# Feed-forward stages of a two-layer hybrid block: VectorE, ScalarE and TensorE keep the written order, high parts three steps ahead and low parts two

## Chip, cores and metric

One core of a Trainium2 chip. The metric is the device time of one execution in microseconds, a median of runs. TensorE does the matrix products, VectorE (DVE) and ScalarE (ACT) prepare their operands, the DMA queues of SyncE (SP) and GpSimd (POOL) bring the weights from HBM.

## What is computed

Two layers on 256 rows of 2048 floats. Layer 0 mixes with a gated delta rule and a gated linear recurrence, layer 1 with two kinds of attention; behind each mixer stands a feed-forward stage of width 5632. The part that matters here:

```python
def swiglu(hn, w_gate, w_up, w_down):
    return (jax.nn.silu(hn @ w_gate) * (hn @ w_up)) @ w_down

for layer in range(2):
    h = h + mixer(rmsnorm(h, norm[layer]), ...)
    h = h + swiglu(rmsnorm(h, ffn_norm[layer]), w_gate[layer], w_up[layer], w_down[layer])
return rmsnorm(h, final_norm)
```

## The kernel before

**Two parts.** Every float32 operand is split into a high part (`whi`, `thi`: a rounding copy on ACT, L181 and L378) and a low part (`wlo`, `tlo`: the rest, a subtraction on DVE, L182 and L379). `Bank.add` (L407) multiplies high by high, high by low and low by high: three matmuls for each of two slices of 128 rows, six for a tile of 128 x 1024 weights and one output bank. The second of the six is the first that reads the low part.

**Blocks.** A feed-forward stage is 11 gu blocks (512 columns of gate and up) and 6 dn blocks (1024 output columns), in three pieces: four gu blocks and two dn blocks twice, then three and two. A block (`block`, L421) has *plain* steps, in which one loaded weight tile feeds two banks (12 matmuls), and *sevens*: two by two tiles of a product by seven block products instead of eight. A seven's seven steps have 6 matmuls each; four of them load a tile, three need a sum of tiles `T` on DVE (L386), and the last one's operand is summed by a DMA that adds in flight (L450, POOL). A gu block has 8 plain steps and two sevens (22 steps; the first block of a stage has 16 plain ones); a dn block has one or two sevens.

**Combinations.** A seven also needs sums and differences of its left operand (`comb`, from `combine`, L389): a sum `cf` of high and low part, four differences `cc`, a high and a low part. For dn blocks the left operand is `hid`, the turned product of the gate and up values, so ten combinations, five for each stage, are made in the middle of the stages.

**The end of a block.** `ends` (L471) joins the banks `M` of the sevens in `e`; then the banks `F` are added, ACT applies silu, DVE multiplies; `turn` (L511) lets TensorE transpose the result (8 transposes, `Ph`, L516), ACT rounds (L520), DVE takes the low part (L521), both into `hid`. Dn blocks add to the residual `h`.

**What sets the order.** A scheduler places the instructions of each engine by priorities and its own estimate; the program's order is its input alone. Only the last lines of the kernel are held in the written order. Buffers: high parts 4 + 2, low parts 3 + 2, raw tiles 3 + 4, banks 4 + 4, `T` 2 (shared with `cc`). A stage's names: `P` plain step, `s1` to `s14` the steps of the two sevens of a gu block.

Of the kernel before, what the change touches and what calls it, by code (L numbers as in the profile page):

```python
# [6 lines left out]
ALU = mybir.AluOpType  # L7
# [40 lines left out]
def body(tc, A, out):  # L48
# [340 lines left out]
    def combine(x4, r=None):  # L389

        f = mx.tile([128, 4, T], F32, name="cf", tag="T", bufs=2)
        c = mx.tile([128, 4, 2, 128], F32, name="cc4", tag="T", bufs=2)
        if r is None:
            r = fp.tile([128, 2, 4, 2, 128], F32R, name="comb", tag="comb", bufs=4)
        V.tensor_tensor(out=f, in0=x4[:, :, 0].bitcast(F32), in1=x4[:, :, 1].bitcast(F32), op=ALU.add)
        a11, a21, a12, a22 = (f[:, 2 * j:2 * j + 2, t * 128:(t + 1) * 128] for j in range(2) for t in range(2))
        for i, (x, y) in enumerate(((a21, a22), (a21, a11), (a22, c[:, 1]), (a12, c[:, 2]))):
            V.tensor_tensor(out=c[:, i], in0=x, in1=y, op=ALU.subtract)
        S.copy(r[:, 0], c)
        V.tensor_tensor(out=r[:, 1], in0=c, in1=r[:, 0].bitcast(F32), op=ALU.subtract)  # L400
        return r

# [14 lines left out]
    def sums():  # L417

        return [[mx.tile([128, 512], F32, name=f"e{t}{i}", tag=f"e{t}{i}", bufs=1) for i in range(2)] for t in range(2)]

    def block(src, x, comb, nd, hooks, tail=0, lead=2, trail=None, pairs=False):  # L421
# [49 lines left out]
        def ends():  # L471
            (c1, w5), (v, w7) = sums()
            S.copy(c1, M[0].t)
            for o, a, b, op in ((v, M[2], c1, ALU.subtract), (w5, M[1], v, ALU.add), (v, M[3], v, ALU.add), (w7, M[3], w5, ALU.add)):
                V.tensor_tensor(out=o, in0=a.t, in1=b, op=op)
            return [[c1, w5], [v, w7]]

# [4 lines left out]
        for j, (i, u) in enumerate(plain):  # L482
# [14 lines left out]
            while k < len(sevens) and k < (j - lead + 2) * len(sevens) // gaps:  # L497
                next(sevens[k])
                k += 1
                if k == len(sevens):  # L500
                    e = ends()

                paused[0] = not more and k < len(sevens)
        return [[y.t for y in f] for f in F], e

    def ffn(L, then, fin=None):

        gu, dn = A[f"gu{L}"], A[f"dn{L}"]
        todo, cx, ch = [], {}, {}

        def turn():  # L511
            Ps = []
            for hid, j, t, a in todo:
                P = ms([128, 4, 128], "Ph")
                for i in range(4):
                    PE.transpose(P[:, i], a[:, i * 128:(i + 1) * 128], tb["ident"])  # L516
                Ps.append((P, hid[:, 4 * j:4 * j + 4, :, t * 128:(t + 1) * 128]))
            todo.clear()
            for P, d in Ps:
                S.copy(d[:, :, 0], P)  # L520
                V.tensor_tensor(out=d[:, :, 1], in0=P, in1=d[:, :, 0].bitcast(F32), op=ALU.subtract)  # L521

        b = 0

        for groups in ((0, 2, 2, 2), (2, 2, 2, 2), (2, 2, 2)):
            piece = len(groups)
            hid = ogp.tile([128, 16, 2, T], F32R, name="hid", tag="hid")
            late = {4: lambda hid=hid: ch.update({0: combine(hid[:, 0:4])})}
            for j in range(piece):
                hooks = {2: turn} if todo else {}  # L530
                if b == 0:
                    hooks[5] = lambda: cx.update({0: combine(X[:, 0:4])})
                    hooks[8] = rstd
                    hooks[10] = lambda: cx.update({1: combine(X[:, 4:8])})
                if j == 1 and piece == 3:

                    hooks[6] = late[4]
                F, e = block(lambda i, u: gu[b, u, i], lambda k: X[:, k], {m: lambda m=m: cx[m] for m in range(groups[j])}, 4, hooks)
                a = e or sums()
                for t in range(2):  # L540
                    if e:
                        V.tensor_tensor(out=a[t][0], in0=F[t][0], in1=e[t][0], op=(ALU.add, ALU.subtract)[t])
                    S.activation(a[t][0], a[t][0] if e else F[t][0], AF.Silu, scale=nrm["rs"][:, t:t + 1])
                for t in range(2):
                    if e:
                        V.tensor_tensor(out=a[t][1], in0=F[t][1], in1=e[t][1], op=ALU.add)
                    V.scalar_tensor_tensor(out=a[t][0], in0=a[t][1] if e else F[t][1], scalar=nrm["rs"][:, t:t + 1],
                                           in1=a[t][0], op0=ALU.mult, op1=ALU.mult)
                    todo.append((hid, j, t, a[t][0]))
                b += 1  # L550
            u0 = 2 * (b - piece)
            for p in range(2):
                end = b == NB and p == 1
                hooks = {2: turn} if todo else {}
                if p == 0 and piece == 4:
                    hooks.update(late)

                    hooks[9] = lambda hid=hid: ch.update({1: combine(hid[:, 4:8])})
                if end and fin:
                    hooks.update({5: lambda: then(0), 6: lambda: then(1)})  # L560
                last = (3, 1, 3) if end and fin else (0, 5 if 4 in hooks else 2)
# [761 lines left out]
```

## Time and profile before

| | us |
|---|---|
| median of 3 runs (2222.97 to 2225.14) | 2224.02 |
| the profiled execution | 2222.2 |
| its span | 2220.4 |

What lies around the span is 1.8 us, and the profiled execution is 1.8 us under the median. How to read the rows further down: times are from the span's start; a matmul's end is modelled, so the pace of TensorE is read from the starts of neighbours; "x2" joins neighbours of one kind, and its time reaches from the first one's start to the last one's end.

### The profile page before, as it was taken

How to read it: one execution, taken by the hardware profiler on the slowest of the kernel's cores; microseconds unless marked ns; L12 is line 12 of the kernel's file. 1: busy time of each engine (PE TensorE's matmuls, PEld its weight loads, DVE VectorE, ACT ScalarE, POOL GpSimd, SP SyncE). 2: the span in 40 equal slices, each digit the busy share in tenths (PEclk: the TensorE clock that was granted, in tenths of full speed). 3: DMA queues.
4: the chain of work that ended last, by engine and by line, in shares of the span. 5: the costliest groups of instructions: out<-in, count | busy, mean ns of one | idle time of the engine just before them, and what ended most of it. 6: DMA issues, size and time to landing. Idle time of an engine off the chain costs nothing.

```text
span 2220.4 us, 30372 instructions
## 1 busy us (share of the span) xinstructions
PE 2206.9 (99%) x10984; PEld 1843.7 (83%) x10984; DVE 1946.1 (88%) x2730; ACT 1302.7 (59%) x1708; POOL 50.6 (2%) x62
## 2 busy tenths in 40 slices
PE   9999999999999999999999999999999999999998
PEld 8888888888888888888888888888888888888886
DVE  8899676679999999999996688857999999999998
ACT  6786664555555665556664554445665566555565
POOL 0000000000000000000000000000000000000000
PEclk9999999999999999999999999999999999999999
DMA  8445446677777776787664455556786777777774
GB/s 282 159 144 169 137 150 190 207 221 228 214 225 230 220 230 217 220 235 225 192 201 152 157 185 172 161 188 200 221 232 212 219 231 231 220 214 239 219 238 150
DMA packets 125991, 451.67 MB, mean 203 GB/s; under 512 B 14064, under 2 KB 15600, under 8 KB 125712
## 3 DMA queue, kind: packets, MB, share of 16 engines
q1 hardware_dynamic: 117488, 420.10, 58.4%
q0 software_dynamic: 8064, 29.36, 7.8%
q8 instruction: 86, 1.41, 0.2%
q14 instruction: 65, 0.53, 0.1%
q10 hardware_dynamic: 288, 0.27, 0.0%
HBM read 447.58 MB, written 2.10 MB: 203 GB/s over the span
## 4 chain that ended last, share of the span: by engine, by line
PE 97%; DVE 2%; DMA 1%; issue 1%; ACT 0%; DVEq 0%; ACTq 0%
PE F L413 16%; PE F L414 16%; PE F L412 16%; PE Pw L201 11%; PE Pw L206 6%; PE M L413 5%; PE M L414 5%; PE M L412 5%; PE Px L305 3%; PE Px L306 3%; PE Px L307 3%; PE Ph L516 1%; PE Psc L1088 1%; PE Pt L328 0%; DVE wlo L182 0%
## 5 line engine op out<-in xcount | busy, mean ns | idle before, releaser
L181 ACT CAST whi<-raw 128x1024 fp32r<-128x1024 f32 x717 | 752.3, 1051 | 640.6 <-PE F L414 279.3
L182 DVE TENSOR_TENSOR wlo<-raw,whi 128x1024 fp32r<-128x1024 f32 x717 | 870.9, 1220 | 153.2 <-PE Px L306 40.9
L201 PE MATMUL Pw<-X,whi 128*128 128x512 f32 x1088 | 388.3, 400 | 0.0
L412 PE MATMUL F<-whi,X 128*128 128x512 f32 x934 | 365.4, 391 | 0.0
L413 PE MATMUL F<-wlo,X 128*128 128x512 f32 x934 | 364.0, 390 | 0.0
L414 PE MATMUL F<-whi,X 128*128 128x512 f32 x934 | 363.6, 389 | 0.0
L206 PE MATMUL Pw<-X,wlo 128*128 128x256 f32 x1088 | 304.7, 280 | 0.1
L378 ACT CAST thi<-T 128x1024 fp32r<-128x1024 f32 x177 | 186.0, 1051 | 123.5 <-DVE T L386 89.4
L201 PEld LDWEIGHTS Pw<-X,whi 128*128 128x128 f32 x1088 | 204.1, 188 | 47.2 <-issue 0.5
L379 DVE TENSOR_TENSOR tlo<-T,thi 128x1024 fp32r<-128x1024 f32 x177 | 216.1, 1222 | 30.8 <-ACT thi L378 30.2
L206 PEld LDWEIGHTS Pw<-X,wlo 128*128 128x128 f32 x1088 | 205.3, 189 | 1.5 <-DVE wlo L182 0.7
L414 PEld LDWEIGHTS F<-whi,X 128*128 128x128 f32 x934 | 175.3, 188 | 36.4
L412 PEld LDWEIGHTS F<-whi,X 128*128 128x128 f32 x934 | 175.3, 188 | 35.8
L413 PEld LDWEIGHTS F<-wlo,X 128*128 128x128 f32 x934 | 175.4, 188 | 35.6
L412 PE MATMUL F<-whi,hid 128*128 128x512 f32 x480 | 187.5, 391 | 0.0
L414 PE MATMUL F<-whi,hid 128*128 128x512 f32 x480 | 186.9, 389 | 0.0
L413 PE MATMUL F<-wlo,hid 128*128 128x512 f32 x480 | 186.9, 389 | 0.0
L386 DVE TENSOR_TENSOR T<-T,raw 128x1024 f32<-128x1024 f32 x118 | 143.9, 1219 | 0.8
L413 PE MATMUL M<-tlo,comb 128*128 128x512 f32 x336 | 131.7, 392 | 0.7 <-DVE tlo L379 0.6
L412 PE MATMUL M<-thi,comb 128*128 128x512 f32 x336 | 131.3, 391 | 0.1
L414 PE MATMUL M<-thi,comb 128*128 128x512 f32 x336 | 131.0, 390 | 0.0
L414 PEld LDWEIGHTS F<-whi,hid 128*128 128x128 f32 x480 | 90.1, 188 | 18.7
(403 smaller groups left out, 3281.0 us busy)
## 6 DMA issues: line engine op xcount, KB each, us to landing
raw<-in_gu SPq DMA_DIRECT2D x352, 512.0 KB, 4.4
raw<-in_dn SPq DMA_DIRECT2D x176, 512.0 KB, 4.3
raw<-in_w0w SPq DMA_DIRECT2D x72, 512.0 KB, 3.7
raw<-in_wo SPq DMA_DIRECT2D x64, 512.0 KB, 3.6
raw<-in_w1w SPq DMA_DIRECT2D x64, 512.0 KB, 3.6
raw<-in_gu POOLq DMA_DIRECT2D x40, 512.0 KB, 7.0
raw<-in_w1x SPq DMA_DIRECT2D x32, 512.0 KB, 4.0
raw<-in_w0x SPq DMA_DIRECT2D x16, 512.0 KB, 3.6
```

The lines of the kernel that those rows point to most:

```text
L181: S.copy(hi, raw)
L182: V.tensor_sub(lo, raw, hi.bitcast(F32))
L201: PE.matmul(P.rearrange("p a b -> p (a b)"), hi[:, kk], X[:, k].rearrange("p a b -> p (a b)"), start=k == 0, stop=False)
L206: PE.matmul(P[:, 0], lo[:, kk], X[:, k, 0], start=False, stop=k == NK - 1)
L305: PE.matmul(Ps[t], x[:, 0, ts], hi[:, kk], start=k == 0, stop=False)
L306: PE.matmul(Ps[t], x[:, 0, ts], lo[:, kk], start=False, stop=False)
L378: S.copy(hi, t)
L379: V.tensor_sub(lo, t, hi.bitcast(F32))
L386: V.tensor_tensor(out=t, in0=a, in1=b, op=ALU.add)
L412: PE.matmul(self.t, xh, hi[:, kk], start=self.i == kk == 0, stop=False)
L413: PE.matmul(self.t, xh, lo[:, kk], start=False, stop=False)
L414: PE.matmul(self.t, xl, hi[:, kk], start=False, stop=kk == 1 and self.i == self.n - 1)
```

## The change

In the feed-forward stages, from the second gu block of a stage up to its last dn block, VectorE, ScalarE and TensorE run in the written order. That order comes from a list: each step gets its high part three steps and its low part two steps before its matmuls stand (`stream`, `ahead`, `low`), and the other work is put between steps at fixed places: the bank sums two steps before a block's end, the F sums one step before and at the end, the product and the transposes one and two steps into the next block, low parts of `hid` and the differences three steps, the low part of the combination four steps in. The steps of a gu block now come as P P P s1 to s4 P s5 to s9 P s10 to s14 P P P, with the transposes of the block before between the second and the third P; before, they stood behind s3: P P s1 s2 s3, transposes, P, s4, P. The last dn block of a stage still goes through `block` and the scheduler, the first gu block through the new list and the scheduler.

Some work is joined or moved: the bank sums are three instructions in place of four, the residual and the product are added on 1024 columns at once, the scale of the up half is an activation on ACT, and a combination of `hid` reads a float copy that ACT takes from the transposes (`e<-Ph`, two for each combination) in place of the sum `cf` on DVE. Such a combination is made in the gu block behind the one that gave its `hid`. The matmuls, transposes and DMAs are the same ones; their order is not.

```diff
-    def combine(x4, r=None):
-        f = mx.tile([128, 4, T], F32, name="cf", tag="T", bufs=2)
+    def combine(f, r=None):
         c = mx.tile([128, 4, 2, 128], F32, name="cc4", tag="T", bufs=2)
...
-        V.tensor_tensor(out=f, in0=x4[:, :, 0].bitcast(F32), in1=x4[:, :, 1].bitcast(F32), op=ALU.add)
...
         S.copy(r[:, 0], c)
+        yield
         V.tensor_tensor(out=r[:, 1], in0=c, in1=r[:, 0].bitcast(F32), op=ALU.subtract)
+    def ends(M):
+        e = sums()
+        S.copy(e[:, 0], M[0].t)
+        V.tensor_tensor(out=e[:, 1], in0=M[2].t, in1=e[:, 0], op=ALU.add)
+        V.tensor_tensor(out=e[:, 2], in0=M[3].t, in1=e[:, 1], op=ALU.add)
+        V.tensor_tensor(out=e[:, 1::2], in0=M[1].t.rearrange("p (a n) -> p a n", a=1).to_broadcast([128, 2, 512]),
+                        in1=e[:, 1:3], op=ALU.subtract)
+    def stream(acts, guard):
...
+        def ahead(n):
+            while at[0] < min(n + 1, len(ready)):
+                y, k = ready[at[0]], at[0]
+                y.raw = y.high()
+                y.hi = (fp.tile([128, 1024], F32R, name="thi", tag="thi", bufs=2) if k % 6 in (1, 4) else
+                        wh.tile([128, 1024], F32R, name="whi"))
+                S.copy(y.hi, y.raw)
+                at[0] += 1
+                if at[0] > 1:
+                    low(at[0] - 2)
...
+        for y in acts:
+            if isinstance(y, Step):
+                if y is guard[0]:
+                    g = tc.manual_schedule(engines={V.engine, S.engine, PE.engine})
+                    g.__enter__()
+                ahead(n + 1 + 2)
+                y.use((y.hi, y.lo))
+                n += 1
+            else:
+                y()
     def ffn(L, then, fin=None):
...
+            def first():
+                a = todo.pop(j)
+                for t in range(2):
+                    P = ms([128, 4, 128], "Ph")
+                    for i in range(4):
+                        PE.transpose(P[:, i], a[:, 2 * t, i * 128:(i + 1) * 128], tb["ident"])
+                    o["P"].append((P, hid[:, 4 * j:4 * j + 4, :, t * 128:(t + 1) * 128]))
+                for P, d in o["P"]:
+                    S.copy(d[:, :, 0], P)
+                if want:
+                    o["f"] = [a[:, 2 * t + 1].rearrange("p (k n) -> p k n", n=128) for t in range(2)]
+                    for t in range(2):
+                        S.copy(o["f"][t], o["P"][t][0])
+            def second():
+                for P, d in o["P"]:
+                    V.tensor_tensor(out=d[:, :, 1], in0=P, in1=d[:, :, 0].bitcast(F32), op=ALU.subtract)
+                if want:
+                    o["c"] = combine(o["f"])
+                    next(o["c"])
+            def third():
+                if want:
+                    ch[j] = run(o["c"])
...
+        for groups, down in (((0, 2, 2, 2), (1, 2)), ((2, 2, 2, 2), (1, 2)), ((2, 2, 2), (1, 1))):
...
+                if late:
+                    add(1, late)
+                if turn:
+                    for n, f in zip((2, 3, 4), turn):
+                        add(n, f)
...
+                    turn = turned(hid, j, j < max(down))
...
+                add(n - 2, bs)
+                add(n - 1, h0)
+                spread(order, put)
+                acts.append(h1)
+        stream(acts, guard)
```

Where it moves instructions: first VectorE, from the last F sums of the second gu block of a stage into the third block, whose steps begin behind them. `e` holds the block's values, `Ph` are the transposes, `T` the sums of a seven. Before:

```order
L546 TENSOR_TENSOR e11_5237<-F11_4959,e11_5237 128x512
L182 TENSOR_TENSOR wlo_5352<-raw_5349,whi_5351 128x1024
L547 SCALAR_TENSOR_TENSOR e10_5236<-e11_5237,rs_4780,e10_5236 128x512
L182 TENSOR_TENSOR wlo_5379<-raw_5376,whi_5378 128x1024
L379 TENSOR_TENSOR tlo_5422<-T_5363,thi_5421 128x1024
L182 TENSOR_TENSOR wlo_5405<-raw4_5402,whi_5404 128x1024
L182 TENSOR_TENSOR wlo_5434<-raw4_5431,whi_5433 128x1024
L386 TENSOR_TENSOR T_5363<-T_5363,raw4_5431 128x1024
L182 TENSOR_TENSOR wlo_5467<-raw_5464,whi_5466 128x1024
L386 TENSOR_TENSOR T_5496<-raw4_5482,raw_5494 128x1024
L521 TENSOR_TENSOR hid_4619<-Ph_5388,hid_4619 128x4x128
L521 TENSOR_TENSOR hid_4619<-Ph_5393,hid_4619 128x4x128
```

Now:

```order
L696 TENSOR_TENSOR e_5280<-F11_5010,e_5280 128x512
L543 TENSOR_TENSOR wlo_5333<-raw_5307,thi_5309 128x1024
L702 TENSOR_TENSOR e_5280<-e_5280 128x2x512
L483 TENSOR_TENSOR T_5352<-raw4_5329,raw_5350 128x1024
L543 TENSOR_TENSOR tlo_5357<-raw4_5329,whi_5331 128x1024
L543 TENSOR_TENSOR wlo_5391<-T_5352,whi_5355 128x1024
L666 TENSOR_TENSOR hid_4619<-Ph_5373,hid_4619 128x4x128
L666 TENSOR_TENSOR hid_4619<-Ph_5378,hid_4619 128x4x128
L396 TENSOR_TENSOR cc4_5407<-e_5280 128x256 x2
L396 TENSOR_TENSOR cc4_5407<-cc4_5407,e_5280 128x256
L396 TENSOR_TENSOR cc4_5407<-e_5280,cc4_5407 128x256
L490 TENSOR_TENSOR T_5352<-T_5352,raw4_5387 128x1024
```

Between the last F sum and the low parts of `hid`, six low parts and two sums `T` stood before; now three low parts, the product and one sum `T`. Behind the low parts of `hid` now stand the four differences of the combination. The rows that follow on VectorE now, up to the plain step behind s4:

```order
L543 TENSOR_TENSOR tlo_5417<-raw4_5387,thi_5389 128x1024
L399 TENSOR_TENSOR comb_5408<-cc4_5407,comb_5408 128x1024
L543 TENSOR_TENSOR wlo_5431<-T_5352,whi_5415 128x1024
L543 TENSOR_TENSOR wlo_5444<-raw4_5427,whi_5429 128x1024
L490 TENSOR_TENSOR T_5352<-T_5352,raw_5440 128x1024
```

These are the low part of s3, the combination's low part, the low parts of s4 and of the plain step. And ScalarE at the same place now (the activations end the second block; `whi_5355` is the high part of s2):

```order
L697 ACTIVATE e_5280<-e_5280,rs_4798 128x512 x2
L530 CAST whi_5331<-raw4_5329 128x1024
L530 CAST whi_5355<-T_5352 128x1024
L657 CAST hid_4619<-Ph_5373 128x4x128
L657 CAST hid_4619<-Ph_5378 128x4x128
L662 COPY e_5280<-Ph_5373 128x512
L662 COPY e_5280<-Ph_5378 128x512
L530 CAST thi_5389<-raw4_5387 128x1024
L397 CAST comb_5408<-cc4_5407 128x1024
L530 CAST whi_5415<-T_5352 128x1024
```

The two copies `e<-Ph` are new; the low parts of `hid` on VectorE wait for them too: both read the same bank, and the program orders them.

## Rows read from the trace of the kernel before

**Rows 1.** The page's head, with TensorE's and VectorE's rows of parts 1 and 2 (the span in 40 slices, tenths) and the granted clock.

```profile
span 2220.4 us, 30372 instructions
PE 2206.9 (99%) x10984; PEld 1843.7 (83%) x10984; DVE 1946.1 (88%) x2730; ACT 1302.7 (59%) x1708; POOL 50.6 (2%) x62
...
PEclk9999999999999999999999999999999999999999
```

**Rows 2.** Busy time of each engine in the two feed-forward stages and in the first 200 us (columns: stretch, its length, busy us and count of PE, PEld, DVE, ACT, POOL, granted clock, DMA share, GB/s).

```profile
430.40:1118.00 687.60, 687.11 (x3080) 566.76 (x3079) 645.86 (x686) 403.41 (x438) 24.32 (x28) 1.00 0.74 222
1521.00:2212.00 691.00, 690.37 (x3084) 569.70 (x3082) 648.30 (x695) 403.68 (x437) 24.15 (x28) 1.00 0.73 220
...
0.00:200.00 200.00, 196.09 (x1342) 172.96 (x1343) 176.48 (x496) 147.62 (x276) 2.11 (x6) 1.00 0.59 192
```

**Rows 3.** The chain of work that ended last: the pieces on VectorE in the feed-forward stages that lie just ahead of a matmul (start, us, what), and two neighbouring matmuls at the fourth of them.

```profile
575.58 1.23 DVE tlo L379
715.45 1.24 DVE tlo L379
966.44 1.22 DVE tlo L379
1803.22 1.24 DVE tlo L379
1866.16 1.22 DVE wlo L182
...
1803.86 0.40 PE L412 MATMUL M<-thi,comb 128*128 128x512 f32 x1
1804.50 0.50 PE L413 MATMUL M<-tlo,comb 128*128 128x512 f32 x1 [0.24 <-DVE tlo L379]
```

**Rows 4.** TensorE in order of time in a gu block: the first and the last of 21 matmuls in a row, and the transposes behind them.

```profile
480.02 0.39 PE L412 MATMUL F<-whi,X 128*128 128x512 f32 x1
...
484.56 0.39 PE L414 MATMUL F<-whi,comb 128*128 128x512 f32 x1
484.78 1.04 PE L516 MATMUL Ph<-tab,e 128*128 128x128 f32 x8
```

**Rows 5.** A turn whose ScalarE was free, in order of time: transposes, high parts, the next matmul, low parts.

```profile
1067.48 1.04 PE L516 MATMUL Ph<-tab,e 128*128 128x128 f32 x8
1068.27 1.05 ACT L520 CAST hid<-Ph 128x512 fp32r<-128x512 f32 x2
1068.27 0.48 PE L412 MATMUL F<-whi,hid 128*128 128x512 f32 x1
1068.88 1.29 DVE L521 TENSOR_TENSOR hid<-Ph,hid 128x512 fp32r<-128x512 f32 x2
```

**Rows 6.** VectorE in order of time, from the last F sum of a gu block to the low parts of its `hid` and on; then differences of combinations elsewhere.

```profile
560.64 0.68 DVE L546 TENSOR_TENSOR e<-F,e 128x512 f32<-128x512 f32 x1
561.24 1.21 DVE L182 TENSOR_TENSOR wlo<-raw,whi 128x1024 fp32r<-128x1024 f32 x1
562.37 0.74 DVE L547 SCALAR_TENSOR_TENSOR e<-e,rs,e 128x512 f32<-128x512 f32 x1
563.04 1.22 DVE L182 TENSOR_TENSOR wlo<-raw,whi 128x1024 fp32r<-128x1024 f32 x1
564.17 1.22 DVE L379 TENSOR_TENSOR tlo<-T,thi 128x1024 fp32r<-128x1024 f32 x1
565.31 2.35 DVE L182 TENSOR_TENSOR wlo<-raw,whi 128x1024 fp32r<-128x1024 f32 x2
567.58 1.22 DVE L386 TENSOR_TENSOR T<-T,raw 128x1024 f32<-128x1024 f32 x1
568.71 1.22 DVE L182 TENSOR_TENSOR wlo<-raw,whi 128x1024 fp32r<-128x1024 f32 x1
569.85 1.22 DVE L386 TENSOR_TENSOR T<-raw,raw 128x1024 f32<-128x1024 f32 x1
570.98 1.28 DVE L521 TENSOR_TENSOR hid<-Ph,hid 128x512 fp32r<-128x512 f32 x2
572.18 1.21 DVE L379 TENSOR_TENSOR tlo<-T,thi 128x1024 fp32r<-128x1024 f32 x1
...
594.48 0.88 DVE L398 TENSOR_TENSOR cc<-cf,cc 128x256 f32<-128x256 f32 x2
...
624.28 0.76 DVE L398 TENSOR_TENSOR cc<-cf 128x256 f32<-128x256 f32 x2
```

**Rows 7.** Groups of instructions by line: the sums `cf` of combinations of `hid`, ScalarE's silu of the gate half (mean ns of one), its high parts, its copies of a bank.

```profile
L395 DVE TENSOR_TENSOR cf<-hid 128x1024 f32<-128x1024 f32 x10 | 12.2, 1220 | 0.0
...
L543 ACT ACTIVATE e<-e,rs 128x512 f32<-128x512 f32 x40 | 28.4, 721 | 17.6 <-DVE e L542 16.9
L520 ACT CAST hid<-Ph 128x512 fp32r<-128x512 f32 x44 | 23.5, 585 | 0.0
```

**Rows 8.** Waits: who waited for whom, us in total, times, longest.

```profile
ACT whi L181 <- PE F L414: 279.3, 228, 4.5
...
ACT whi L181 <- DMA raw<-in_gu: 19.0, 19, 2.4
...
PE Pgate L673 <- ACT cx L610: 0.6, 1, 0.6
```

**Rows 9.** DMA issues: tensor, queue, count, size, median us from issue to landing.

```profile
raw<-in_gu SPq DMA_DIRECT2D x352, 512.0 KB, 4.4
raw<-in_dn SPq DMA_DIRECT2D x176, 512.0 KB, 4.3
...
raw<-in_gu POOLq DMA_DIRECT2D x40, 512.0 KB, 7.0
```

More of the change, by code (lines that the diff above doesn't have):

```diff
@@ new lines, in stream, with low @@
+    def stream(acts, guard):
+        ready = [y for y in acts if isinstance(y, Step)]
+        at = [0, 0]
+        g = None
+        def ahead(n):
[8 more added lines that the diff above has]
+                    low(at[0] - 2)
+            while at[1] < min(n, len(ready)):
+                low(at[1])
+        def low(k):
+            if k < at[1]:
+                return
+            y = ready[k]
+            y.lo = (fp.tile([128, 1024], F32R, name="tlo", tag="tlo", bufs=2) if k % 5 in (1, 3) else
+                    wl.tile([128, 1024], F32R, name="wlo"))
+            V.tensor_sub(y.lo, y.raw, y.hi.bitcast(F32))
+            at[1] = k + 1
+        n = 0
+        for y in acts:
[8 more added lines that the diff above has]
+                y()
+        if g is not None:
+            g.__exit__(None, None, None)
@@ L508, in ffn @@
         gu, dn = A[f"gu{L}"], A[f"dn{L}"]
[L509 to L521, printed above, removed]
@@ new lines, in spread, with values, bank_sums, half @@
+        def spread(order, put):
+            for n, y in enumerate(order):
+                acts.extend(put.get(n, []))
+                acts.append(y)
+        def values(hid, j, F, M, ns):
+            o = {}
+            rs = lambda t: nrm["rs"][:, t:t + 1]
+            def bank_sums():
+                o["a"] = ends(M) if ns else sums()
+            def half(i):
+                def f():
+                    for t in range(2):
+                        v = o["a"][:, 2 * t + i]
+                        if ns:
+                            V.tensor_tensor(out=v, in0=F[t, i].t, in1=v, op=ALU.add)
+                        S.activation(v, v if ns else F[t, i].t, AF.Copy if i else AF.Silu, scale=rs(t))
+                return f
+            def product():
+                a = o["a"]
+                V.tensor_tensor(out=a[:, 0::2], in0=a[:, 1::2], in1=a[:, 0::2], op=ALU.mult)
+                todo[j] = a
+            return bank_sums, half(0), half(1), product
@@ L526, in ffn @@
+        b, late, turn = 0, None, None
+        for groups, down in (((0, 2, 2, 2), (1, 2)), ((2, 2, 2, 2), (1, 2)), ((2, 2, 2), (1, 1))):
             piece = len(groups)
             hid = ogp.tile([128, 16, 2, T], F32R, name="hid", tag="hid")
[L528 to L550, printed above, removed]
@@ new lines, in ffn @@
+        stream(acts, guard)
+        if fin:
+            hooks, last = {5: lambda: then(0), 6: lambda: then(1)}, (3, 1, 3)
+        else:
+            hooks, last = {}, ()
+            then(0)
+            then(1)
+        F, e = block(lambda i, u: dn[2 + i, 2 * (b - piece) + u], lambda k: hid[:, k], {m: lambda m=m: ch[m] for m in range(down[1])},
+                     piece, hooks, *last)
+        for t in range(2):
+            et = e[:, 2 * t:2 * t + 2].rearrange("p a n -> p (a n)")
+            V.tensor_tensor(out=et, in0=h[:, t, 1024:2048], in1=et, op=ALU.add)
```

173 lines of the change are left out of this document (130 added, 43 removed).

## The prediction

> **What bounds the kernel now.** I read the page's head first. TensorE is busy for 2206.9 of 2220.4 us, at the full clock in every slice [rows 1]. [...] In order of time, 21 matmuls in a row start 0.227 us apart: (484.78 − 480.02) / 21 [rows 4]. I call this the pace; at it a plain step of 12 matmuls takes 2.72 us and a step of a seven 1.36 us. TensorE leaves it at five places only, and those are the five VectorE pieces of the chain of waits [rows 3]. At the fourth of them neighbours start 0.64 apart, 0.41 more than the pace. With 0.41 for each of the five, all stalls of both stages are worth 2.1 us at most. So the change can win 2 us, under 0.1%; about 0.2%, or 4.4 us, is what a measurement of this kernel can tell from no change. What it can lose is not bounded so, since VectorE, now in a fixed order, has less than 7% of spare time.
>
> **Work that goes, comes and moves.** ScalarE has 403 us of work in a stage of 690 [rows 2], so it counts by its place in the queue and not by its sum. All these edits lie beside TensorE's saturated stream and enter the sum with nothing.
> - Ten sums `cf` go from VectorE, 12.2 us [rows 7]. In their place ScalarE takes 20 copies `e<-Ph`, each like its rounding copy of the same bank, 0.585 [rows 7].
> - The 44 scalings of the up half become activations, 0.72 each by the silu [rows 7]. The two products of 0.74 become one on 1024 columns. Three bank sums in place of four move the same columns.
> - The DMAs are the same. The slowest, the adding one on POOL's queue, lands after 7.0 us at the median [rows 9]; it starts behind the sum of s2 and is wanted for the high part of s7, five steps of a seven and a plain one later, 9.5 us. SP's loads land in 4.4 us. They start when a low part frees a raw tile, so VectorE's lag passes to them; seven raw tiles lie ahead of it.
>
> What is gone is cover: if VectorE falls behind, TensorE waits in full, since nothing of its own may be pulled forward any more.
>
> **The place that I think decides.** In the order of now, the third block of a stage begins with this on VectorE: last F sum, a low part, the product, a sum `T`, the low parts of s1 and s2, two low parts of `hid`, four differences, `T` of s4, low part of s3, low part of the combination, low parts of s4 and of the plain step. Before, six low parts and two sums stood between the last F sum (560.64) and the low parts of `hid` (570.98) [rows 6]. That was a lead of several steps; now it is used up while VectorE waits for the turn.
>
> I worked this out as a timetable, zero being the start of TensorE's last step of the preceding block. Start-to-start times of VectorE are 0.60 for 512 columns and about 1.135 for 1024 [rows 6]. Of two differences that follow each other, the second starts some 0.33 to 0.45 behind the first [rows 6].
> 1. The last matmul of F starts at 2.72 − 0.227 and lasts 0.39 [rows 4]; with 0.04 to hand over (1804.46 to 1804.50 [rows 3]), the last F sum starts at 2.93. Behind it 0.60 and five instructions of 1.135: VectorE is through with s2's low part at 9.2.
> 2. TensorE goes through two plain steps until 8.16 and then makes the transposes. ScalarE's copy starts 0.79 after them (1067.48 to 1068.27 [rows 5]), at 8.95, and there are four copies now, two of them new. Two in a row took 1.05 [rows 5], so 0.475 from start to start. The third ends at 8.95 + 0.95 + 0.585 = 10.49. The low part of `hid` reads the same bank, and the program orders it behind that copy: it starts at 10.53, and VectorE has stood still for 1.3 us.
> 3. Two low parts (1.20), four differences (three of 0.335, one of 0.45), the sum `T` (1.135): 14.32. The low part of s3 is done at 15.54 and seen by TensorE at 15.58.
> 4. TensorE has meanwhile done the third plain step (8.95 to 11.67), s1 and s2 (to 14.39). The second matmul of s3 wants the low part at 14.62. **It waits 0.95 us.**
> 5. Next on VectorE come the combination's low part and that of s4: seen at 17.85. TensorE, already late, wants it at 15.58 + 5 × 0.227 + 0.227 = 16.94. **It waits 0.90 us.**
> 6. The low part of the plain step behind s4 is seen at 18.98, and TensorE wants it at 19.21: no wait. The rest of the block gives VectorE its lead back.
>
> So each combination of `hid` costs 1.86 us of TensorE's time. A block without one has neither copies nor differences: the low part of s3 is then done at 13.1, 1.5 us before it is wanted. There are ten combinations [rows 7], five a stage, made in the gu blocks behind the first and second of a piece and, in the third piece, behind the first. That is 18.6 us. The trace of before has no such wait, so its price is an estimate. From below, if the low parts of `hid` need not stand behind the new copies, they start 0.95 sooner, the wait in s3 goes and that in s4 stays: 9 us for ten. From above, with every dependent difference at its 0.44 [rows 6] and VectorE's 1.22 in place of 1.135 for four more instructions of the path, 2.5 us a block: 25. I take 18.6, since each of its terms is a row.
>
> The other term is the five old stalls, some of which the fixed lead of two steps takes away: −2.0 (between 0 and −2.1). For the mixers I count nothing: their order on TensorE hardly moves. **Sum: 2222.2 + 18.6 − 2.0 = 2238.8 for the profiled execution; that one is 1.8 under the median, so 2241 against the median.** Its own range, from the two bounds: 2224.0 + 9 − 2 to 2224.0 + 25, that is 2231 to 2249.
>
> **The rivals.**
> - *Still slower: ScalarE's queue is blocked by a late load.* ScalarE waited for a gu tile 19 times, 2.4 us at the longest [rows 8], and the scheduler could let other work pass. Now the copy of bank sums, the activations and the turn's copies queue behind such a wait, and VectorE's sums and low parts behind those. With about 1 us (19.0 / 19) in each of 10 to 20 gu blocks on top: 2251 to 2261. For it: three steps of a seven are 4.1 us, and the median landing is 4.4 [rows 9]. Against it: SP starts a load as soon as one of seven raw tiles is free, more than the three steps need.
> - *Not slower: the low part of s3 comes in time.* The point from which it decides: VectorE must be 0.95 us earlier at s3 and 1.85 at s4, so that TensorE never leaves its pace. It would take that the copies don't hold the low parts of `hid`, and that another 0.9 us of VectorE's work before s4 goes faster than in [rows 6]. Then the old stalls alone change: 2222 to 2224. For it: over a whole block VectorE has less work than before, some 41.5 us against 41.6 of TensorE. Against it: VectorE cannot start on the F sums before TensorE ends the block, and every piece up to s4 comes from a row.
> [...]
> - *Faster.* The feed-forward stages can give 2.1 us as long as the pace stays 0.227. A faster pace would be needed, and the inside of a step doesn't change. [...]
>
> **Chances.** Forecast 0.73, still slower 0.10, not slower 0.13, the clock 0.02, faster 0.02. From these: slower by over 0.2% 0.73 + 0.10 + 0.02 = 0.85, within 0.2% 0.13, faster 0.02. The range takes the forecast's own 2231 to 2249 and the still slower case up to near its end; some room below is left for a part of the ten blocks without waits: 2227 to 2260. Left out are not slower, the clock and faster, 0.17.
>
> **What would show it.** Right: in the waits of now TensorE stands about 20 times for low parts from VectorE, some 0.9 us each, in s3 and s4 of five gu blocks of a stage (the second and third, the sixth and seventh, the tenth), and next to nowhere else; ahead of each, VectorE waits about 1.3 us for the turn; clock 1.00; VectorE some 20 us less busy than 1946.1, ScalarE some 35 more; span about 2237. Step 2 is wrong if the low parts of `hid` start before the new copies end; steps 3 to 5 are wrong if the waits lie in other steps or in blocks without a combination; the sum is wrong if TensorE waits for high parts or loads, or falls below its pace with no wait.

## The result, and the profile after

Six runs of the changed kernel have a median of 2239.86 us (2239.06 to 2241.06), six of the kernel before 2223.56. The ratio is 1.0073, 95% interval 1.0060 to 1.0086: slower by 16.3 us, where 2241 was predicted. The profiled execution took 2239.82 us, its span is 2237.9, 17.5 more than before.

The head of the page, beside [rows 1]:

```profile
span 2237.9 us, 30514 instructions
PE 2211.5 (99%) x10984; PEld 1843.4 (82%) x10984; DVE 1939.3 (87%) x2640; ACT 1324.2 (59%) x1772; POOL 50.6 (2%) x62
...
PEclk9999999999999999999999999999999999999999
```

The same two stretches as in [rows 2], each of which now ends before its stage does:

```profile
430.40:1118.00 687.60, 681.50 (x3045) 560.47 (x3045) 634.51 (x637) 410.08 (x466) 24.31 (x28) 1.00 0.74 220
...
1521.00:2212.00 691.00, 683.85 (x3049) 562.34 (x3048) 635.62 (x637) 412.31 (x465) 24.17 (x28) 1.00 0.75 222
```

TensorE was busy for all but 0.5 us of the first before the change; now 6.1 are missing, at the same clock. TensorE's waits in the feed-forward stages say for what (engine, line, what it waited for: total, times, longest):

```profile
PE M L418 <- DVE wlo L543: 3.6, 6, 0.6
PE F L418 <- DVE wlo L543: 3.6, 6, 0.6
...
PE M L418 <- DVE tlo L543: 2.4, 4, 0.6
PE F L418 <- DVE tlo L543: 2.4, 4, 0.6
PE F L417 <- DVE h L720: 1.1, 1, 1.1
```

Twenty waits for low parts, in s3 and s4 (`F` and `M`) of ten blocks. They add up to 12 us in this view, but a wait costs more than it shows. TensorE in order of time, s3 and s4 of the third block of the first stage:

```profile
531.47 0.39 PE L417 MATMUL F<-thi,comb 128*128 128x512 f32 x1
532.45 0.50 PE L418 MATMUL F<-tlo,comb 128*128 128x512 f32 x1 [0.59 <-DVE tlo L543]
532.79 0.40 PE L419 MATMUL F<-thi,comb 128*128 128x512 f32 x1
...
533.71 0.39 PE L417 MATMUL M<-whi,comb 128*128 128x512 f32 x1
534.72 0.50 PE L418 MATMUL M<-wlo,comb 128*128 128x512 f32 x1 [0.62 <-DVE wlo L543]
```

From start to start the first wait takes 0.98 in place of 0.227, 0.76 lost before rounding (0.76 or 0.78 in all twenty), and the matmul behind it comes 0.34 later, 0.11 lost. That is 0.875 a wait, 1.75 a combination, 17.5 for the twenty. To balance this, all distances more than 0.1 above the pace have to be counted in the same way, those at transposes left out: the two stages lose 3.0 us by them before the change and 19.8 now. The 19.8 are the 17.5, another 1.4 where the written order ends (below) and 0.9 in small pieces; the 3.0 hold the five old stalls [rows 3], which are gone. The difference is 16.8 of the 17.5. Of the rest, 0.4 lies ahead of the first feed-forward stage.

VectorE ahead of those waits, from the last F sums to the low part of the plain step behind s4, beside [rows 6]:

```profile
519.57 1.28 DVE L696 TENSOR_TENSOR e<-F,e 128x512 f32<-128x512 f32 x2
520.76 1.22 DVE L543 TENSOR_TENSOR wlo<-raw,thi 128x1024 fp32r<-128x1024 f32 x1
521.90 1.22 DVE L702 TENSOR_TENSOR e<-e 128x1024 f32<-128x1024 f32 x1
523.03 1.22 DVE L483 TENSOR_TENSOR T<-raw,raw 128x1024 f32<-128x1024 f32 x1
524.17 1.22 DVE L543 TENSOR_TENSOR tlo<-raw,whi 128x1024 fp32r<-128x1024 f32 x1
525.46 1.23 DVE L543 TENSOR_TENSOR wlo<-T,whi 128x1024 fp32r<-128x1024 f32 x1
527.37 1.29 DVE L666 TENSOR_TENSOR hid<-Ph,hid 128x512 fp32r<-128x512 f32 x2 [0.69 <-ACT e L662]
528.58 0.75 DVE L396 TENSOR_TENSOR cc<-e 128x256 f32<-128x256 f32 x2
529.25 0.42 DVE L396 TENSOR_TENSOR cc<-cc,e 128x256 f32<-128x256 f32 x1
529.70 0.42 DVE L396 TENSOR_TENSOR cc<-e,cc 128x256 f32<-128x256 f32 x1
530.04 1.22 DVE L490 TENSOR_TENSOR T<-T,raw 128x1024 f32<-128x1024 f32 x1
531.18 1.22 DVE L543 TENSOR_TENSOR tlo<-raw,thi 128x1024 fp32r<-128x1024 f32 x1
532.31 1.22 DVE L399 TENSOR_TENSOR comb<-cc,comb 128x1024 fp32r<-128x1024 f32 x1
533.45 1.22 DVE L543 TENSOR_TENSOR wlo<-T,whi 128x1024 fp32r<-128x1024 f32 x1
534.58 1.22 DVE L543 TENSOR_TENSOR wlo<-raw,whi 128x1024 fp32r<-128x1024 f32 x1
```

ScalarE at the same place, beside [rows 5]; the high part of s3 (`thi`) stands behind the four copies:

```profile
525.77 1.07 ACT L657 CAST hid<-Ph 128x512 fp32r<-128x512 f32 x2 [0.35 <-PE Ph L654]
526.73 1.09 ACT L662 COPY e<-Ph 128x512 f32<-128x512 f32 x2
527.69 1.08 ACT L530 CAST thi<-raw 128x1024 fp32r<-128x1024 f32 x1
```

Read against the timetable: TensorE's last step of the block before starts at 516.97, the zero. The low part of `hid` starts at 10.40 (10.53 forecast). The low part of s3 ends at 532.40, and TensorE goes on at 15.48 (15.58); behind s4's low part at 17.75 (17.85). It is the same in every one of the ten blocks: counted from its transposes, the low part of `hid` starts at 10.40 and the low part of s3 ends at 15.43.

The last row of the waits lies where the written order ends and the scheduler's block begins, at the end of the second stage:

```profile
2196.28 0.39 PE L417 MATMUL M<-whi,hid 128*128 128x512 f32 x1
2197.81 0.50 PE L417 MATMUL F<-whi,hid 128*128 128x512 f32 x1 [1.14 <-DVE h L720]
```

The new block's F bank waits for VectorE's residual sums (`h`, L720), which stand behind the two joined ones of 1.22 us.

### The profile page after: what moved, and what is told of

It reads as the page before. It is cut to its first block, busy times and chain, and to the rows that moved or that the text cites. A ratio compares the mean times of both kernels' runs of the same rounds, so it can differ in the third digit from the quotient of the medians.

```text
span 2237.9 us, 30514 instructions
## 1 busy us (share of the span) xinstructions
PE 2211.5 (99%) x10984; PEld 1843.4 (82%) x10984; DVE 1939.3 (87%) x2640; ACT 1324.2 (59%) x1772; POOL 50.6 (2%) x62
## 4 chain that ended last, share of the span: by engine, by line
PE 93%; DVE 4%; issue 1%; ACT 1%; DMA 0%; DVEq 0%; ACTq 0%
PE F L418 16%; PE F L419 16%; PE F L417 16%; PE Pw L201 11%; PE Pw L206 5%; PE M L418 4%; PE M L419 4%; PE M L417 4%; PE Px L305 3%; PE Px L306 3%; PE Px L307 3%; DVE wlo L543 1%; PE Ph L654 1%; DVE cc L396 1%; DVE T L490 1%
## 5 line engine op out<-in xcount | busy, mean ns | idle before, releaser
L181 ACT CAST whi<-raw 128x1024 fp32r<-128x1024 f32 x267 | 279.6, 1051 | 278.9 <-PE Pw L201 83.6
L182 DVE TENSOR_TENSOR wlo<-raw,whi 128x1024 fp32r<-128x1024 f32 x267 | 325.6, 1221 | 116.4 <-PE Px L306 38.2
L530 ACT CAST whi<-raw 128x1024 fp32r<-128x1024 f32 x334 | 343.4, 1047 | 56.7 <-PE F L419 40.2
L417 PE MATMUL F<-whi,X 128*128 128x512 f32 x698 | 272.9, 391 | 0.0
L419 PE MATMUL F<-whi,X 128*128 128x512 f32 x698 | 272.2, 390 | 0.0
L543 DVE TENSOR_TENSOR wlo<-raw,whi 128x1024 fp32r<-128x1024 f32 x198 | 240.7, 1220 | 17.3 <-PE F L418 7.8
L418 PE MATMUL F<-wlo,X 128*128 128x512 f32 x646 | 252.5, 391 | 0.1
L530 ACT CAST whi<-T 128x1024 fp32r<-128x1024 f32 x110 | 116.1, 1055 | 200.3 <-DVE T L490 110.4
L530 ACT CAST thi<-raw 128x1024 fp32r<-128x1024 f32 x170 | 177.8, 1047 | 27.0 <-PE F L419 19.8
L543 DVE TENSOR_TENSOR tlo<-raw,whi 128x1024 fp32r<-128x1024 f32 x136 | 165.9, 1220 | 11.3 <-PE F L418 6.0
L417 PEld LDWEIGHTS F<-whi,X 128*128 128x128 f32 x698 | 131.1, 188 | 27.0
L419 PEld LDWEIGHTS F<-whi,X 128*128 128x128 f32 x698 | 131.1, 188 | 26.7
L418 PE MATMUL F<-tlo,X 128*128 128x512 f32 x374 | 146.1, 391 | 0.2 <-DVE tlo L379 0.2
L543 DVE TENSOR_TENSOR wlo<-raw,thi 128x1024 fp32r<-128x1024 f32 x102 | 124.4, 1220 | 4.7 <-PE F L418 3.0
```

Source lines behind the costliest of these rows:

```text
L181: S.copy(hi, raw)
L182: V.tensor_sub(lo, raw, hi.bitcast(F32))
L417: PE.matmul(self.t, xh, hi[:, kk], start=self.i == kk == 0, stop=False)
L418: PE.matmul(self.t, xh, lo[:, kk], start=False, stop=False)
L419: PE.matmul(self.t, xl, hi[:, kk], start=False, stop=kk == 1 and self.i == self.n - 1)
L530: S.copy(y.hi, y.raw)
```

## Experiments

Ratios are to the kernel before, run beside each; times are medians. "Lost" is a distance of neighbouring starts less 0.227.

**Turn one step later.** VectorE's low parts of `hid` and differences pass behind the low part of s3.

```diff
-                    for n, f in zip((2, 3, 4), turn):
+                    for n, f in zip((2, 4, 5), turn):
```

> The low parts of hid and the differences are put one step later (position 4 in place of 3), the low part of the combination at 5. Forecast's theory (the place in VectorE's queue decides): the sum T of s4 and the low part of s3 now pass ahead of the turn, so the waits in s3 and s4 go (20 times 0.88 us, from the starts of neighbours); but the combination's low part now stands right ahead of that of the plain step behind s4, whose second matmul then waits about 0.75 us. 2239.9 - 17.7 + 7.5 = 2230 (2226 to 2233). Rival (VectorE has too little time over a whole block, wherever its work stands): the waits only move, 2238 to 2242. Rival (TensorE's new order of steps, s1 to s4 in a row): 2238 to 2242.

2242.91 us, 1.0091 (1.0076 to 1.0106), above both expectations. No wait in s3 any more, but 0.82 lost in s4 and 0.85 in the plain step behind it. My expectation failed, and the rows say why. VectorE, then ScalarE:

```profile
526.61 1.23 DVE L490 TENSOR_TENSOR T<-T,raw 128x1024 f32<-128x1024 f32 x1
528.94 1.23 DVE L543 TENSOR_TENSOR tlo<-raw,thi 128x1024 fp32r<-128x1024 f32 x1 [1.10 <-ACT thi L530]
530.08 1.28 DVE L666 TENSOR_TENSOR hid<-Ph,hid 128x512 fp32r<-128x512 f32 x2
```

```profile
526.87 1.10 ACT L662 COPY e<-Ph 128x512 f32<-128x512 f32 x2
527.83 1.08 ACT L530 CAST thi<-raw 128x1024 fp32r<-128x1024 f32 x1
```

VectorE no longer stands still for the turn, but for s3's high part, which ScalarE still has behind the turn's copies. I had moved the work in one queue and not looked at the other.

**The same, with the combination's low part at position 17.**

```diff
+                    for n, f in zip((2, 4, 17), turn):
```

> As the run before, but the low part of the combination at position 17, among the last plain steps of the block. Forecast's theory: no wait in s3, s4 or the plain step behind them; 2222 (2220 to 2226). Rival (VectorE has too little time over a block): waits in other steps, s5 to s9 or at the block's end, 2230 to 2242.

2248.72 us, 1.0114 (1.0099 to 1.0129). 0.82 in s4, 0.66 in the plain step, and 0.43 to 0.75 at the block's end, where the moved low part now stands. The time is above both expectations. It looked as if a gu block had no room for a combination anywhere; the run with one step more, below, shows that it need not have.

**The sum on VectorE again, no copies.** The sum reads `hid`, high and low, into the same `e`.

```diff
-                        S.copy(o["f"][t], o["P"][t][0])
...
+                        V.tensor_tensor(out=o["f"][t], in0=d[:, :, 0].bitcast(F32), in1=d[:, :, 1].bitcast(F32), op=ALU.add)
```

> The combination's float values come from a sum of high and low part of hid on VectorE (two of 512 columns) in place of ScalarE's two copies. Forecast's theory: the low parts of hid start about 0.7 us sooner, but the sums take 1.2 us, so the low part of s3 is 0.4 to 0.5 us later; ten times: 2244 (2242 to 2246). Rival (the copies on ScalarE, and the wait for them, are the cause): the lag shrinks by 0.7 us to 0.95 us each, 2230 to 2234.

2243.90 us, 1.0094 (1.0079 to 1.0109): as the theory had it. The loss in s3 grows from 0.76 to 1.10 (1.39 in one block), that in s4 stays. So the copies are not the cause: without them the loss stays, and the sum in their place costs more.

**A plain step between s3 and s4 again.**

```diff
-            order += sevens[g * len(sevens) // (mid + 1):(g + 1) * len(sevens) // (mid + 1)]
+            cut = [0, 3, 9, 14] if (len(sevens), mid) == (14, 2) else [k * len(sevens) // (mid + 1) for k in range(mid + 2)]
+            order += sevens[cut[g]:cut[g + 1]]
```

> A plain step stands between s3 and s4 again (s1 to s3, P, s4 to s9, P, s10 to s14). Forecast's theory: VectorE's lag of about 1.8 us stays, since the work put ahead is the same; the low part of s3 comes in time (T of s4 stands behind it now), and the plain step behind s3 waits 1.8 us in one piece: 2239 (2236 to 2242). Rival (s1 to s4 in a row on TensorE are the cause): 2222 to 2226.

2241.74 us, 1.0085 (1.0068 to 1.0102). Ten single waits, 1.71 to 1.74 lost, in the plain step behind s3, as expected:

```profile
533.27 0.39 PE L417 MATMUL F<-whi,X 128*128 128x512 f32 x1
535.24 0.50 PE L418 MATMUL F<-wlo,X 128*128 128x512 f32 x1 [1.58 <-DVE wlo L544]
```

With the plain step moved, VectorE's lag is paid in another place and not saved. Other orders of TensorE's steps were not tried.

**The scheduler in place of the written order.**

```diff
-                if y is guard[0]:
+                if y is None:
```

> The written order is not entered: the same program, joined sums, copies and places in the list are left to the scheduler. Theory (the fixed order makes VectorE wait for the turn and holds low parts behind it): the pairs of waits in s3 and s4 go or shrink below 0.4 us each, 2222 to 2228. Rival (the lead of two low parts and the combination in a full gu block cost the time, in whatever order): 2234 to 2245.

2232.05 us, 1.0043 (1.0028 to 1.0058), between both. The pairs are gone; 14 stalls of 0.16 to 1.4 lie scattered, and 2.1 at the end of the second stage. The largest of the 14 are four of 1.03 for low parts and three of 0.5 to 1.4 for high parts. So the order costs some 8 us against the scheduler's on the same program, and the program costs the other 9 with the scheduler too, by these stalls, which I did not follow up.

**The combination on GpSimd.**

```diff
-            V.tensor_tensor(out=c[:, i], in0=x, in1=y, op=op)
+            E.tensor_tensor(out=c[:, i], in0=x, in1=y, op=op)
...
+                    o["c"] = combine(o["f"], E=G)
```

> The four differences and the low part of the ten combinations run on GpSimd, all else as in the change. VectorE then has the two low parts of hid, T and the low part of s3 in a row: 1.45 us sooner, s4's 2.6 us sooner. Theory (VectorE's work between the turn and the low parts of s3 and s4 is what TensorE waits for): all 20 waits go, 2222 (2220 to 2226). Rival (the turn itself comes too late, whatever follows it): waits of 0.5 us or more stay in s3 and s4, 2230 to 2240. If VectorE and GpSimd hold each other up, VectorE's instructions beside the differences are longer than 1.22 us and part of the gain goes.

2287.12 us, 1.0288 (1.0271 to 1.0306), above both expectations. GpSimd's work, and what VectorE and ScalarE do meanwhile:

```profile
532.20 2.41 POOL L396 TENSOR_TENSOR cc<-e 128x256 f32<-128x256 f32 x2 [2.58 <-ACT e L662]
534.57 1.73 POOL L396 TENSOR_TENSOR cc<-cc,e 128x256 f32<-128x256 f32 x1
536.37 0.74 POOL L396 TENSOR_TENSOR cc<-e,cc 128x256 f32<-128x256 f32 x1
538.27 2.35 POOL L399 TENSOR_TENSOR comb<-cc,comb 128x1024 fp32r<-128x1024 f32 x1 [1.16 <-ACT comb L397]
```

```profile
533.94 1.76 DVE L543 TENSOR_TENSOR tlo<-raw,thi 128x1024 fp32r<-128x1024 f32 x1
539.17 2.54 DVE L543 TENSOR_TENSOR wlo<-T,whi 128x1024 fp32r<-128x1024 f32 x1 [3.48 <-ACT whi L530]
```

```profile
537.15 1.04 ACT L397 CAST comb<-cc 128x1024 fp32r<-128x1024 f32 x1 [4.16 <-POOL cc L396]
538.10 1.04 ACT L530 CAST whi<-T 128x1024 fp32r<-128x1024 f32 x1
```

The combination's high part waits on ScalarE for the slow differences, and s4's high part stands behind it; s4's low part then takes 2.54. TensorE loses over 2 us twice in every such block. With these waits the clock fell: 1.00 up to the first of them, then (windows across them, and behind):

```profile
536.90:541.50 4.60, 1.15 (x3) 0.29 (x1) 2.33 (x1) 3.88 (x4) 2.57 (x2) 0.75 0.28 99
541.50:545.50 4.00, 3.74 (x9) 2.97 (x10) 3.94 (x5) 1.41 (x2) 0.00 (x0) 0.50 0.38 110
```

The run tells nothing of the theory, since it puts a new wait in the same place, but it shows the cost of one queue's wait for another.

**The copies behind s3's high part.** Transposes at 2, the four copies at 3, low parts of `hid` and differences at 4, both halves of the combination at 12.

```diff
-            return [first, second, third]
+            return [first, copies, second, third]
...
+                    for n, f in zip((2, 3, 4, 12), turn):
```

> After the first two runs: ScalarE's high part of s3 stood behind the four copies of the turn, so VectorE waited 1.1 us for it in place of the turn. Here the four copies stand behind that high part (position 3), low parts of hid and differences at 4, high and low part of the combination at 12. Theory (what counts is that neither engine stands still ahead of s4): VectorE no longer waits; low part of s4 at 15.8 against 16.0 wanted, so no or little wait: 2222 to 2229. Rival (a gu block with a combination asks for more of VectorE's time than TensorE takes, 41.4 of work against 41.6 with not a gap allowed): the wait moves behind s4 and to the block's end, 2232 to 2242.

2231.98 us, 1.0043 (1.0028 to 1.0058), above the theory's range and at the lower end of the rival's. All 20 waits in s3 and s4 are gone; in eight of the ten blocks 0.52 is lost in s10 and 0.8 in a plain step behind it, right after position 12 (0.4 in the other two). There VectorE waits 0.49 for the combination's high part, which I had put at the same position, and 1.14 of low part follows. So with low parts two ahead the combination's low part was paid at its new place in the gu block, too.

**The combinations in the dn blocks.** Order and lead stay; VectorE sums `cf` again, the copies go, the first dn block's seven begins later.

```diff
-                                        {m: lambda m=m: ch[m] for m in range(down[p])}, piece, 3, 3)
+                                        {m: lambda m=m: ch[m] for m in range(down[p])}, piece, *(((5, 2), (7, 3))[piece - 3] if p == 0 else (3, 3)))
+                    if p == 0:
+                        for c, n in ((0, piece * 2 - 3), (1, 13))[:max(down)]:
+                            for f in made(hid, c):
+                                add(n, f)
+                                n += 1
```

> The written order stays; the ten combinations are made in the dn blocks, with the sum cf on VectorE (the copies on ScalarE go), the seven of the first dn block begins two or four plain steps later. A dn block has about 9 us of VectorE's time to spare, a gu block behind a turn has then 38.9 us of work in 41.6. Theory (fixed order is harmless where the work fits, and the loss is the combination's place): all 20 waits go, 2222 (2220 to 2227). Rival (the written order itself costs TensorE time at each turn): 2234 to 2240.

2227.56 us, 1.0020 (1.0010 to 1.0029), just above the theory's range. The 20 waits are gone, and the time is 12 us under the change. What is left stands in the dn blocks of the third piece: 2.5 us lost in the first stage, where a bank waits for VectorE's late residual sums; in the second stage 1.9 for a low part behind the combination (the turn there came late, since ScalarE first waited 4.25 for the load of the final norm's weights) and 0.9 and 1.0 at the end. Behind the wait of 2.5 the granted clock was 0.55 for 3.7 us (1093.3 to 1097.0), and 1.00 again behind that; over the profiled execution it was 0.997, where the kernel before has 0.999.

**The differences twice.**

```diff
+        for i, x, y, op in n * ((0, a21, a22, ALU.subtract), ...
...
-                    o["c"] = combine(o["f"])
+                    o["c"] = combine(o["f"], n=2)
```

> The four differences of each of the ten combinations run twice at their place (the second time the same values). Theory (VectorE's queue ahead of the low part of s3 sets the time): 1.45 us more in s3, ten times, 2239.9 + 14.5 = 2254.4 (2252 to 2257); the wait in s3 is then 2.3 us, as long as single waits behind which matmuls came 0.43 us apart for a while in the two runs before, so with the lower clock for 6 to 9 matmuls each time up to 2272. Rival (VectorE waits for the turn in any case and has room for it): 2240 to 2243.

2259.43 us (2256.07 to 2262.22), 1.0165 (1.0151 to 1.0179): above the 2252 to 2257 without the lower clock, and below the 2272 with it. The wait in s3 in the same block as above, 0.59 there:

```profile
535.63 0.50 PE L418 MATMUL F<-tlo,comb 128*128 128x512 f32 x1 [2.05 <-DVE tlo L543]
```

The loss in s3 goes from 0.76 to 2.22, 1.46 more for 1.45 of work; s4 keeps 0.78. In the profiled execution (2256.1, granted clock 0.998 over the whole) one such wait of the ten was followed by matmuls 0.43 apart; the other executions are up to 6 us longer, at 0.995 and 0.996. So VectorE's work there is paid one for one, and what is above that goes with the clock.

**One step more.** High parts four steps and low parts three ahead.

```diff
-                ahead(n + 1 + 2)
+                ahead(n + 1 + 3)
```

> High parts four steps and low parts three ahead of the matmuls, all else as in the change. So high and low part of s3 and the sum T of s4 stand ahead of the turn. Theory after the runs so far (a gu block with a combination holds 41.4 us of VectorE's work and about 2 us of gaps, so it lasts 43.3 us at best, against 41.7): the waits move behind s4 and the time is 2230 to 2236. Rival (the lead of two steps is what was too short): 2221 to 2226.

2223.91 us, 1.0006 (0.9997 to 1.0015): not to be told from the kernel before, and 16 us under the change. My theory after the first runs, that a gu block with a combination lasts 43.3 us because it is full, falls; the rival that the lead of two was too short is what was measured. The block is full all the same: from one product (`e<-e`) to the next VectorE takes 42.68 us in the third block, 0.47 of it waiting, while TensorE needs 41.69 from turn to turn where it loses nothing. But it need not fit by itself. The longer lead covers the lack, and the next block, which has no combination, gives it back (39.53). Where two such blocks follow each other, 0.9 us is still lost in the second. VectorE at the place of the rows above, without a wait, with the two products around it, then ScalarE:

```profile
520.76 1.22 DVE L702 TENSOR_TENSOR e<-e 128x1024 f32<-128x1024 f32 x1
...
523.15 1.22 DVE L490 TENSOR_TENSOR T<-T,raw 128x1024 f32<-128x1024 f32 x1
524.29 1.22 DVE L543 TENSOR_TENSOR tlo<-raw,thi 128x1024 fp32r<-128x1024 f32 x1
525.43 1.28 DVE L666 TENSOR_TENSOR hid<-Ph,hid 128x512 fp32r<-128x512 f32 x2
...
563.44 1.21 DVE L702 TENSOR_TENSOR e<-e 128x1024 f32<-128x1024 f32 x1
```

```profile
520.78 1.04 ACT L530 CAST thi<-raw 128x1024 fp32r<-128x1024 f32 x1
522.76 1.07 ACT L657 CAST hid<-Ph 128x512 fp32r<-128x512 f32 x2 [0.94 <-PE Ph L654]
```

VectorE has the same order here as with the turn one step later (`T`, low part of s3, then `hid`). There, s3's high part stood behind the turn's copies on ScalarE and VectorE waited 1.10; here it stands ahead of them.

**High parts four ahead, low parts two.** In this run the low parts of the steps that read a sum `T` are taken after `T` has gone on to its next sum, so that part of the computation differs and its result is not the kernel's; VectorE, ScalarE and TensorE have the same number of instructions.

```diff
-                if at[0] > 1:
-                    low(at[0] - 2)
-            while at[1] < min(n, len(ready)):
+                if at[0] > 2:
+                    low(at[0] - 3)
+            while at[1] < min(n - 1, len(ready)):
...
-                ahead(n + 1 + 2)
+                ahead(n + 1 + 3)
```

> High parts (and with them the sums T) four steps ahead, low parts two as in the change: half of the run with one step more. On ScalarE the high part of s3 then stands ahead of the four copies; on VectorE T of s4 stands ahead of the turn, but the low parts of s3 and s4 stay behind it, and T of s6 comes in ahead of the low part of the plain step. Theory (it takes both, VectorE's low parts and ScalarE's high parts ahead of the turn; neither alone): no wait in s3, about 0.65 in s4 and 0.8 in the plain step, with 0.11 each behind them, 1.65 a combination: 2238 (2235 to 2241). Rival (the place of ScalarE's high parts is what the run with one step more gained by): 2222 to 2228.

2236.84 us, 1.0061 (1.0044 to 1.0078). 0.66 lost in s4 and 0.90 in the plain step behind it, nothing in s3, as the theory had it. The high parts' half of the extra step alone gives back 3 of the 16 us. For the low parts' half stands the turn one step later, which gives VectorE the same order there and gives back none. Both together give all.

**The dn blocks, third piece changed.** The combinations stay in the dn blocks. In the third piece the seven begins one plain step later than in the change, in place of two, with three plain steps behind it, and the combination is made one step sooner. Against the change:

```diff
-                                        {m: lambda m=m: ch[m] for m in range(down[p])}, piece, 3, 3)
+                                        {m: lambda m=m: ch[m] for m in range(down[p])}, piece, *(((4, 3), (7, 3))[piece - 3] if p == 0 else (3, 3)))
+                    if p == 0:
+                        for c, n in ((0, {3: 2, 4: 5}[piece]), (1, 13))[:max(down)]:
```

> As the combinations in the dn blocks, but in the third piece the seven begins one plain step later than in the change, not two, and the combination is made one step sooner; three plain steps stand at the end again. Theory: the late bank sums at the end of that block (2.5 and 1.9 us, with the clock at the lower level behind them) were the rest of that run's loss; without them and without the five old stalls 2221 to 2223, so the kernel before within 0.2%. Rival (the written order costs something at the ends of a stage, where it meets the scheduler): 2225 to 2229.

2220.64 us (2219.97 to 2222.05, 11 runs), just under what was expected; 0.9991, interval 0.9982 to 1.0000. (The expectation puts both long stalls of the run before down to bank sums; as told above, one was a low part.) That is 19 us under the change and 2 under the kernel before, at the edge of what can be told from none. Its span is 2218.0, and of TensorE's waits in the feed-forward stages the view shows one:

```profile
PE F L417 <- DVE h L723: 0.8, 1, 0.8
```

## Why the prediction was right

**What bounds the kernel: right.** The two stages meant are those of [rows 2], where VectorE had 6.1% and 6.2% of spare time. The most that the change could win was put at 2.1 us. By the starts of neighbours it was somewhat more, 3.0: TensorE left its pace by 0.11 to 0.13 at twelve other places too, five of them right behind a stall. Of the two best versions, one lies 1.2 us above the kernel before and one 2.1 under it.

**The place and the steps 1 to 6: right.** Each time of the timetable from step 2 on was met within 0.15 us. The ten blocks and the two steps of each are the forecast ones, and behind s4 there is no wait. The low part of s3 in a block without a combination, forecast to be done at 13.1, ends at 12.98 in the block behind the two. One step was off without effect: VectorE was through with s2's low part at about 9.5 and not 9.2, since that one waits 0.15 for ScalarE's high part of `T` (in the block shown, 9.7: its last F sum came late, too). So it stood still for 0.7 to 1.0 at the turn in eight of the blocks and for 2.0 in the second block of each stage, not for 1.3, and the end of the wait is set by ScalarE all the same.

**The sizes: 17.5 for 18.6, −1.6 for −2.0.** A combination costs 1.75. The forecast 1.86 came from delays of 0.95 and 0.90; measured are 0.76 and 0.77, and 0.11 behind each, a term that was not there. The wait in s3 is shorter since the low part ends 0.11 sooner and TensorE comes 0.11 later (the plain step behind the transposes takes 2.82, not 2.72). The −1.6 is by the forecast's measure, the waiting matmul alone. At the end of the second stage 1.3 us had not been forecast. These errors have both signs and offset each other in part, so the nearness of 2239.9 to 2241 is partly luck; the mechanism is not. There is luck in the 1.8 us, too, that the forecast put between the profiled execution and the median: now the two agree, and for the profiled one 2238.8 was forecast, 1.0 too low.

**Both bounds of the wait held.** The lower one needed the low parts of `hid` free of the copies; the row shows them waiting for the copy (0.69 for `e`), and so it is in all ten blocks. The sum on VectorE instead brought 4 us more, so the copies were the cheaper way.

**The rivals.** *Still slower*: ScalarE's waits for a load did not reach TensorE here; in the run with the combinations in the dn blocks one did, with 1.9 us lost. *Not slower*: the point given, VectorE 0.95 us sooner at s3 and 1.85 at s4, is passed with one step more (3.9 and 2.4 sooner in the third block, counted from the transposes), at 2223.9. *The clock*, given 0.02: not in the change, whose stretches stay at 1.00, but in runs with longer waits; with the combination on GpSimd, whose waits lose over 2 us, the window above has 0.50. *Faster*: the pace stayed 0.227.

**Off the path.** In the page's busy time, where instructions that overlap count once, VectorE fell by 6.8 us, not 20, and ScalarE rose by 21.5, not 35. With the times of all instructions added up, VectorE fell by 23 and ScalarE rose by 42, nearer to the forecast, which had added up instructions too. Nothing hung on either.

**What is shown and what is argued.** Shown: VectorE's work ahead of the low part of s3 is paid one for one (differences twice), and the loss goes when the work is taken from there (dn blocks) or the lead is one step longer. Shown, too: VectorE's part of that lead alone is not enough, nor ScalarE's (turn one step later, high parts four ahead). The run with high parts four ahead also puts the sum `T` of s6 ahead of the plain step's low part, so not all of its loss there must come from the short lead. Not settled: why the scheduler, given the new program, still loses 9 us.

## What to carry to other kernels

Where the bounding engine has no slack, a written order should be read queue by queue at the one place where another engine's answer is awaited: add up what stands behind that wait until the next piece the bounding engine wants. Lead must be given on every queue of the chain; moving work in VectorE's queue gained nothing while ScalarE's still held the high part behind the same turn. Before rearranging, try the lead itself: one number gave back all of the loss here that the runs can tell. A block that asks for a little more of an engine than it has time for is no loss as long as the lead covers it and the next block gives it back.

## What the runs showed of the hardware

- TensorE's twenty waits in the change cost about 0.27 us more each than the waits view shows: 0.60 there, 0.875 by the starts of neighbours, 0.11 of it at the matmul behind.
- With ten single waits of 1.7 us (the plain step between s3 and s4) TensorE's granted clock was 0.999 over the run, as in the kernel before. Behind some waits of 2.1 to 2.5 us it fell, and matmuls came some 0.43 us apart: 0.50 in the window of 4.0 us above (the combination on GpSimd, 0.985 over the profiled execution) and 0.55 for 3.7 us (the first run with combinations in the dn blocks). Behind nine of the ten waits of 2.22 with the differences twice they did not (0.998 over the profiled execution).
- In the block shown, VectorE's low part, 1.22 us elsewhere, took 1.76 and 2.54 beside GpSimd's subtractions, and GpSimd's difference, 0.74 with VectorE waiting, took 1.73 beside VectorE. No run shows what holds them up.
